# A hybrid encoder step on one core: split weights are kept in DRAM after their first use

## Chip, core and metric

The kernel runs on one core of a Trainium2 chip. Its metric is the device time of one execution in microseconds (us): 2907.6 us before, the median of three runs (2906.4 to 2909.33).

## What is computed

One layer of a streaming encoder is applied to 2048 prompt tokens and 32 sample tokens of width 1024. The parts that matter here, from the reference:

```python
h = _rmsnorm(x, g_mix)
u = h @ w_in                                   # queries, keys, values, pooling input
att = _stick_breaking(q, k_all, v_all, q_pos, k_pos)
x = x + jnp.concatenate([att, pool], axis=-1) @ w_out
h2 = _rmsnorm(x, g_ffn)
x = x + (jax.nn.silu(h2 @ w_ffn_gate) * (h2 @ w_ffn_up)) @ w_ffn_down
gate = jax.nn.sigmoid(_rmsnorm(x, g_ple) @ w_ple_gate)
x = x + (p @ w_ple) * gate
```

w_out and w_ple_gate are 1024 x 1024, w_ffn_gate and w_ffn_up 1024 x 2816, w_ffn_down 2816 x 1024, all float32. A final norm follows.

## The kernel before, in words

**Products in three terms.** Every large product is made from operands split in two float32r parts, hi and lo: `mm3` (lines 204 to 208) issues hi·hi, hi·lo and lo·hi into one PSUM bank. An operand is split by a cast to float32r on ScalarE (ACT), which gives hi, and a subtraction, on VectorE (DVE) with few exceptions on GpSimd (POOL), which gives lo.

**Blocks.** The 2080 tokens are columns. The input projection and pooling branch (`project`) take six blocks of up to 384 columns, the part behind the attention (`rest`) six blocks of 336 or 352, in three pairs each. All blocks of `project` come first. The attention is not a stage of its own: `drive` weaves its steps between the products of the later projections and of the first two pairs of `rest`. In the third pair there is no attention left. One pair of `rest` does, in order: the output projection, one block after the other; the FFN for both blocks together, in groups of up to four chunks of 128 hidden columns; the per-layer embedding with its gate; the final norm, which runs in the background of the next pair. In the last pair the embedding goes one block after the other.

**Weights.** A weight piece is 128 partitions x 1024 elements (0.5 MB). `plan_col` and `plan_down` put pieces into `wplan` in the order of use; `wunit` (lines 183 to 193) hands out one piece and starts the piece after it. A piece is loaded into one of three `wraw` buffers by a DMA from SP's queue (line 95), cast into one of three `whi` (line 190) and subtracted into one of three `wlo` (line 191). A pair of `rest` uses 16 pieces of w_out (eight per block), 22 of w_ffn_gate, 22 of w_ffn_up, 22 of w_ffn_down, and 8 of w_ple_gate (16 in the last pair). So w_out is loaded and split six times and each FFN weight three times. The input projection uses 16 pieces of w_in per pair. A piece of w_out serves 24 matmuls (eight chunks, three terms, one block), a piece of the FFN 48.

**Order of the work.** PE's instructions keep the order in which they are written. The other engines and SP's queue are put in order by the Tile scheduler; each engine then works in order. All DMAs stand in SP's queue: weights, keys and values for the attention (`kt`, `vt`, `q`), the sixteen activation tiles that a pair's output projection starts with (`as<-hx`, line 868), the residual rows (`xs`) and the stores of results. A matmul that needs a PSUM bank waits until its last reader is done; a buffer of a weight is written again when PE has done its last matmul on it.

Of the kernel before, what the change touches and what calls it, by code (L numbers as in the profile page):

```python
# [9 lines left out]
F32 = mybir.dt.float32  # L10
# [7 lines left out]
KC = D // 128  # L18
# [15 lines left out]
# token columns: the 32 sample tokens first, then the prompt.  # L34
# blocks of the input projection (whole tiles of the prompt) and of the rest
# [7 lines left out]
# query groups that a pair of blocks waits for  # L43
# [22 lines left out]
def pieces(c0, n):  # L66
    """Runs of at most 128 tokens in the columns [c0, c0 + n), sample and prompt apart."""
    out, off = [], 0
    if c0 == 0:
        out.append((0, DSEQ))  # L70
        off = DSEQ
    while off < n:
        out.append((off, min(128, n - off)))
        off += 128
    return out
# [3 lines left out]
def stickbreak_step(  # L79
# [35 lines left out]
    # one bank is a third one for transposes while the input projection runs,  # L115
    # and a fourth one for the products after that
# [27 lines left out]
    # gains of the norms, features on partitions  # L144
# [33 lines left out]
    # Weights come in pieces of [128, a, b] with a*b = 1024, in a known order, each  # L178
    # split into two float32r parts; LOOK of them are emitted ahead of their use.
    wplan = collections.deque()  # L180
    wready = collections.deque()

    def wunit():
        while wplan and len(wready) <= LOOK:
            src, a, b, eng = wplan.popleft()
            raw = wpool.tile([128, a, b], F32, tag="wraw", name=nm("wraw"), bufs=RAW_BUFS)
            dma(raw, src)
            hi = wpool.tile([128, a, b], F32R, tag="whi", name=nm("whi"), bufs=W_BUFS)
            lo = wpool.tile([128, a, b], F32R, tag="wlo", name=nm("wlo"), bufs=W_BUFS)
            S.copy(hi, raw)  # L190
            eng.tensor_sub(lo, raw, hi.bitcast(F32))  # L191
            wready.append((hi, lo))
        return wready.popleft()
# [4 lines left out]
    def plan_col(w, c, eng=V):  # L198
        wplan.append((kmaj(w[0, :, c:c + 128]), KC, 128, eng))
# [4 lines left out]
    def mm3(ps, a, b, first=True, last=True):  # L204
        """ps += a.T @ b with a, b = (hi, lo) pairs of APs."""
        T.matmul(ps, a[0], b[0], start=first, stop=False)  # L206
        T.matmul(ps, a[0], b[1], start=False, stop=False)  # L207
        T.matmul(ps, a[1], b[0], start=False, stop=last)  # L208

    # Dense work is a generator that yields PE time; `defer` emits something  # L210
    # after so many further accumulation groups, so that PE does not wait for it.
# [26 lines left out]
    def col_sums(accs, tiles, dim):  # L238
        """accs [128, n]: their sum over partitions, tokens on partitions -> 1/rms [128, nt]."""
        nt = len(tiles)  # L240
        ss = small.tile([128, 4], F32, tag="ss", name=nm("ss"))
        bank = tp_bank()
        if any(wd < 128 for _, wd in tiles):
            GP.memset(ss[:, :nt], 1.0)
        for i, (off, wd) in enumerate(tiles):
            for k, a in enumerate(accs):
                T.matmul(bank[:wd, i:i + 1], a[:, off:off + wd], ones[:, 0:1], start=k == 0, stop=k == len(accs) - 1)
        i = 0
        while i < nt:
            j = i  # L250
            while j < nt and tiles[j][1] == tiles[i][1]:
                j += 1
            wd = tiles[i][1]
            V.tensor_scalar(ss[:wd, i:j], bank[:wd, i:j], 1.0 / dim, EPS, op0=ALU.mult, op1=ALU.add)
            i = j
        return rsqrt_cols(ss, nt)
# [6 lines left out]
    def bcast(r, tiles, n, out):  # L263
        """r [token, tile] -> out [128, n], the same on every partition."""
        bank = tp_bank()
        c0 = tiles[0][0]
        for i, (off, wd) in enumerate(tiles):
            T.matmul(bank[:, off - c0:off - c0 + wd], r[:wd, i:i + 1].broadcast_to([wd, 128]), ident[:wd, :wd],
                     start=True, stop=True)
        S.copy(out, bank[:, :n])  # L270

# [7 lines left out]
    VSC = dram.tile([PAST, NH, 128], F32R, name="vsc")  # L279

# [4 lines left out]
    def rows(c, wd, sample, prompt):  # L285
        """Token rows of a sample / prompt array for the columns from c."""
        if c < DSEQ:
            return sample[c:c + wd, :]
        return prompt[c - DSEQ:c - DSEQ + wd, :]

# [1 line left out]
    halo_prev = [None]  # L292

    def open_block_pair(sup, xpool, pool):
        """The inputs of two blocks: rows on their way, the transposes as a queue to run."""
# [3 lines left out]
        def load_x(b):  # L299
            for i, (off, wd) in enumerate(st["TL"][b]):  # L300
                # the first pair has room where the pooling branch will be
                tag, bufs = ("yt", 2) if b == 1 and i > 0 else ("xn", 4)
                xn = pool.tile([128, D], F32, tag=tag, name=nm("xn"), bufs=bufs)
                dma(xn[:wd, :], rows(st["C0"][b] + off, wd, x_sample[0], x_prompt[0]))
                st["xs"][b].append(xn)
# [34 lines left out]
    def project(sup, pool, st, following):  # L340
        """following() opens the next pair."""
# [33 lines left out]
        for half in range(2):  # L375
            for j in range(2):
                c = 2 * SBW + 256 * half
                wplan.append((kmaj(w_in[0, 512 * j:512 * (j + 1), c:c + 256]), 4, 256, V))
# [6 lines left out]
        # (first column in up, first column of the block, columns)  # L385
# [14 lines left out]
        def pooled(b, g, ps):  # L400
            """The windows of one channel group, from its projection in PSUM; then its map, later."""
# [73 lines left out]
        # the first group goes along with the transposes of x  # L475
# [51 lines left out]
        # values, tokens on partitions  # L527
# [24 lines left out]
        # keys and queries, features on partitions  # L552
# [18 lines left out]
        for c in range(8):  # L571
# [5 lines left out]
            for b in sup:  # L577
# [4 lines left out]
                if last and not isk and c >= HAND_OVER:  # L582
                    # the pools of this phase close as early as possible
                    u = ap.tile([128, WMAX], F32, tag="bot", name=nm("u"), bufs=3)[:, :N[b]]
                    uu = ap.tile([128, 2, WMAX], F32R, tag="aa", name=nm("aa"), bufs=3)[:, :, :N[b]]
                else:
                    u, uu = tmp(b, "u", 3), pair(b)
# [36 lines left out]
    def attn_units(gi, qc, qws, segs):  # L624
        """Per head and key segment of a group of query tiles (columns from qc, widths qws):
        query-tile parts and key-tile parts as closures, in pipeline order."""
# [137 lines left out]
    def attention():  # L764
        """Yields (projections needed, cost) before each slot."""
# [78 lines left out]
    def rest(sup, pool, apool):  # L844
# [7 lines left out]
        def slot(b):  # L852
            """A tile of two float32r parts: [128, 2, N]."""
            return apool.tile([128, 2, OMAX], F32R, tag="as", name=nm("as"), bufs=ACT_SLOTS)[:, :, :N[b]]
# [23 lines left out]
        def ready_h(b, c, key):  # L878
            """X chunk c is final: its squares, and its product with the gain in two parts."""
# [17 lines left out]
        def plan_down(fs):  # L897
            n = 1024 // len(fs)
            for c in range(0, D, n):
                wplan.append((kmaj(w_down[0, fs[0] * 128:(fs[-1] + 1) * 128, c:c + n]), len(fs), n, V))  # L900

        for b in sup:
            for oc in range(KC):
                plan_col(w_out, oc * 128)
        for i, fs in enumerate(groups):
            for f in fs:
                plan_col(w_gate, f * 128)
                plan_col(w_up, f * 128)
# [3 lines left out]
        for i in range(KC if sup != OS[-1] else 2 * KC):  # L912
            plan_col(w_pgate, (i % KC) * 128, V if i else GP)
# [4 lines left out]
        # output projection, one block after the other  # L918
# [18 lines left out]
        # gated FFN  # L937
# [65 lines left out]
        def embed_in(b):  # L1003
            """The embedding's input, transposed."""
# [23 lines left out]
        # per-layer embedding; the last pair goes one block after the other, so that  # L1028
        # the final norm of its first block runs beside the second
# [60 lines left out]
        # the final norm of the last block: the left half of its rows is transposed and  # L1090
        # multiplied by the gain before the sums of squares are known
# [39 lines left out]
        # final norm, back to rows  # L1131
# [89 lines left out]
```

## Time and profile before

| | |
|---|---|
| median of three runs | 2907.6 us (2906.4 to 2909.33) |
| profiled execution, time and span | 2909.9 us, from the first instruction to the last |
| busy: PE, DVE, ACT, POOL | 97%, 70%, 45%, 22% |
| DMA | 366.50 MB in 521919 packets, mean 126 GB/s |
| granted clock of PE | 0.991 of full speed |

Busy time is the time in which at least one instruction of the engine runs. Matmuls overlap, so the mean duration of one (some 320 ns) is longer than the time from one to the next. In the views, L95 is line 95 of the kernel, `whi<-wraw` an instruction that writes a tile whi from a tile wraw, and a wait names the engine that waits, and behind the arrow what ended the wait. PEclk is the share of full clock that TensorE was granted; DMA share is the mean busy share of the core's 16 DMA engines.

### The profile page before, as it was taken

How to read it: one execution, taken by the hardware profiler on the slowest of the kernel's cores; microseconds unless marked ns; L12 is line 12 of the kernel's file. 1: busy time of each engine (PE TensorE's matmuls, PEld its weight loads, DVE VectorE, ACT ScalarE, POOL GpSimd, SP SyncE). 2: the span in 40 equal slices, each digit the busy share in tenths (PEclk: the TensorE clock that was granted, in tenths of full speed). 3: DMA queues.
4: the chain of work that ended last, by engine and by line, in shares of the span. 5: the costliest groups of instructions: out<-in, count | busy, mean ns of one | idle time of the engine just before them, and what ended most of it. 6: DMA issues, size and time to landing. Idle time of an engine off the chain costs nothing.

```text
span 2909.9 us, 50174 instructions
## 1 busy us (share of the span) xinstructions
PE 2829.9 (97%) x18478; PEld 2783.4 (96%) x18478; DVE 2023.3 (70%) x3498; ACT 1302.7 (45%) x2829; POOL 635.8 (22%) x1175
## 2 busy tenths in 40 slices
PE   7989889999999999999999999999999999999998
PEld 6989889989999999998999999999999999999998
DVE  6456689888887787887888777777655644444466
ACT  4454566665444444455554444444343422222243
POOL 2002224223312222232332211212132211111120
PEclk9999999999999999999999999999999999999999
DMA  6775766793333323323563333333225522222223
GB/s 190 207 222 161 188 196 180 219 270 107 98 114 94 104 87 100 109 82 110 185 190 87 90 119 103 105 99 98 82 80 164 172 69 70 67 72 66 73 85 124
DMA packets 521919, 366.50 MB, mean 126 GB/s; under 512 B 62653, under 2 KB 508925, under 8 KB 521674
## 3 DMA queue, kind: packets, MB, share of 16 engines
q1 hardware_dynamic: 521674, 363.30, 42.3%
q8 instruction: 146, 2.39, 0.4%
q14 instruction: 99, 0.81, 0.1%
HBM read 292.89 MB, written 70.32 MB: 125 GB/s over the span
## 4 chain that ended last, share of the span: by engine, by line
PE 81%; DVE 9%; issue 4%; DMA 3%; ACT 2%; POOL 1%; SPq 0%; DVEq 0%; POOLq 0%; ACTq 0%
PE mm L206 23%; PE mm L207 22%; PE mm L208 22%; PE z L694 4%; PE tp L723 4%; PE av L737 2%; PE av L736 2%; DVE keep L712 2%; DVE wlo L191 1%; DVE as L883 1%; DVE win L417 1%; DVE beta L713 1%; ACT whi L190 1%; DVE aa L176 1%; DMA kt<-ks 1%
## 5 line engine op out<-in xcount | busy, mean ns | idle before, releaser
L206 PE MATMUL mm<-as,whi 128*128 128x352 f32 (+1 forms) x3936 | 1299.7, 330 | 2.5 <-DMA as<-hx 2.5
L207 PE MATMUL mm<-as,whi 128*128 128x352 f32 (+1 forms) x3936 | 1264.1, 321 | 0.0
L208 PE MATMUL mm<-as,wlo 128*128 128x352 f32 (+1 forms) x3936 | 1259.3, 320 | 0.0
L206 PEld LDWEIGHTS mm<-as,whi 128*128 128x128 f32 x3936 | 740.9, 188 | 4.9 <-DMA as<-hx 3.8
L207 PEld LDWEIGHTS mm<-as,whi 128*128 128x128 f32 x3936 | 740.9, 188 | 0.3 <-DVE as L883 0.3
L208 PEld LDWEIGHTS mm<-as,wlo 128*128 128x128 f32 x3936 | 740.9, 188 | 0.0
L190 ACT CAST whi<-wraw 128x1024 fp32r<-128x1024 f32 x326 | 342.5, 1051 | 488.7 <-PE mm L207 458.4
L191 DVE TENSOR_TENSOR wlo<-wraw,whi 128x1024 fp32r<-128x1024 f32 x323 | 395.6, 1225 | 79.2 <-ACT whi L190 78.0
L712 DVE TENSOR_TENSOR_SCAN keep<-keep,keep,zeros 128x384 f32<-128x384 f32 (+2 forms) x328 | 315.9, 963 | 115.0 <-ACT keep L697 114.2
L697 ACT ACTIVATE keep<-z 128x384 f32<-128x384 f32 (+3 forms) x464 | 195.8, 422 | 364.7 <-PE z L694 315.0
L967 POOL TENSOR_TENSOR sg<-sg,t 128x352 f32<-128x352 f32 (+1 forms) x132 | 157.9, 1197 | 729.1 <-ACT sg L942 718.2
L713 DVE TENSOR_TENSOR beta<-beta,keep 128x384 f32<-128x384 f32 (+3 forms) x464 | 236.0, 509 | 29.7 <-POOL keep L709 0.5
L709 POOL COPY keep<-keep 128x1 f32<-128x1 f32 (+1 forms) x328 | 149.0, 454 | 437.2 <-DVE keep L712 436.2
L694 PE MATMUL z<-kt,q 128*128 128x384 f32 (+4 forms) x928 | 211.8, 309 | 17.3 <-ACT beta L698 10.7
L176 DVE TENSOR_TENSOR aa<-tp,aa 128x384 fp32r<-128x384 f32 (+4 forms) x472 | 213.0, 451 | 16.5 <-ACT aa L175 15.9
L175 ACT CAST aa<-tp 128x384 fp32r<-128x384 f32 (+4 forms) x472 | 193.1, 409 | 65.6 <-PE tp L723 55.8
L940 DVE TENSOR_TENSOR t<-mm,rbc 128x352 f32<-128x352 f32 (+1 forms) x180 | 92.7, 515 | 162.3 <-PE mm L208 156.8
L206 PE MATMUL mm<-hh,whi 128*128 128x384 f32 (+2 forms) x576 | 202.1, 351 | 3.2 <-ACT acc L447 2.6
L988 DVE TENSOR_TENSOR xs<-xs,mm 128x352 f32<-128x352 f32 (+1 forms) x288 | 144.1, 509 | 85.6 <-PE mm L208 84.9
L723 PE MATMUL tp<-ident,beta 128*128 128x128 f32 (+1 forms) x1112 | 199.0, 273 | 0.6 <-DVE aa L176 0.6
L698 ACT ACTIVATE beta<-z 128x384 f32<-128x384 f32 (+3 forms) x464 | 194.4, 419 | 0.0
L207 PE MATMUL mm<-hl,whi 128*128 128x384 f32 (+2 forms) x576 | 188.9, 328 | 0.6 <-DVE hl L328 0.5
(155 smaller groups left out, 3749.2 us busy)
## 6 DMA issues: line engine op xcount, KB each, us to landing
wraw<-in_w_ffn_gate_dram SPq DMA_DIRECT2D x66, 512.0 KB, 3.9
wraw<-in_w_ffn_up_dram SPq DMA_DIRECT2D x66, 512.0 KB, 3.9
wraw<-in_w_ffn_down_dram SPq DMA_DIRECT2D x66, 512.0 KB, 3.5
wraw<-in_w_in_dram SPq DMA_DIRECT2D x48, 512.0 KB, 4.7
wraw<-in_w_out_dram SPq DMA_DIRECT2D x48, 512.0 KB, 5.3
kt<-ks SPq DMA_DIRECT2D x112, 192.0 KB, 2.4
vt<-vs SPq DMA_DIRECT2D x112, 192.0 KB, 2.8
wraw<-in_w_ple_gate_dram SPq DMA_DIRECT2D x32, 512.0 KB, 3.9
```

Of the source, the lines that this page charges most:

```text
L176: V.tensor_sub(lo, src, hi.bitcast(F32))
L190: S.copy(hi, raw)
L191: eng.tensor_sub(lo, raw, hi.bitcast(F32))
L206: T.matmul(ps, a[0], b[0], start=first, stop=False)
L207: T.matmul(ps, a[0], b[1], start=False, stop=False)
L208: T.matmul(ps, a[1], b[0], start=False, stop=last)
L694: T.matmul(z[:qw, :wi], hd["q"][:, e, qsl], un["k"][:, :wi], start=(e == 0), stop=(e == 1))
L697: S.activation(keep[:qw, :wi], z[:qw, :wi], AF.Sigmoid, scale=-0.125)
L698: S.activation(beta[:qw, :wi], z[:qw, :wi], AF.Sigmoid, scale=0.125)
L712: V.tensor_tensor_scan(rev, rev, zeros[:qw].broadcast_to([qw, wi]), initial=init, op0=ALU.mult, op1=ALU.add)
L713: V.tensor_mul(beta[:qw, :wi], beta[:qw, :wi], keep[:qw, 1:wi + 1])
L723: T.transpose(bank[:kw, qo[i]:qo[i] + qws[i]], un["b"][i][:qws[i], k0:k0 + kw], ident[:qws[i], :qws[i]])
```

## The change

Both parts of a piece now share one tile `w` of 128 x 2 x 1024 elements, again with three buffers. A piece with a key is split at its first use as before, and then stored with both parts (1 MB) in a DRAM tile of its own in `WS2`. When the same key comes again, both parts are loaded straight into `w` (1 MB), with neither a raw load nor a cast nor a subtraction. Keys name the matrix and its first column (for w_ffn_down also its first row chunk), so each of 82 pieces (8 of w_out, 66 of the FFN, 8 of w_ple_gate) is split once; w_in has no keys. The second block of the first pair is the first to load pieces of w_out ready. Comments are removed too.

```diff
     wplan = collections.deque()
     wready = collections.deque()
+    wkept = {}

     def wunit():
         while wplan and len(wready) <= LOOK:
-            src, a, b, eng = wplan.popleft()
-            raw = wpool.tile([128, a, b], F32, tag="wraw", name=nm("wraw"), bufs=RAW_BUFS)
-            dma(raw, src)
-            hi = wpool.tile([128, a, b], F32R, tag="whi", name=nm("whi"), bufs=W_BUFS)
-            lo = wpool.tile([128, a, b], F32R, tag="wlo", name=nm("wlo"), bufs=W_BUFS)
-            S.copy(hi, raw)
-            eng.tensor_sub(lo, raw, hi.bitcast(F32))
-            wready.append((hi, lo))
+            src, a, b, eng, key = wplan.popleft()
+            w = wpool.tile([128, 2, a, b], F32R, tag="w", name=nm("w"), bufs=W_BUFS)
+            if key in wkept:
+                dma(w, wkept[key].rearrange("p c (a b) -> p c a b", a=a))
+            else:
+                raw = wpool.tile([128, a, b], F32, tag="wraw", name=nm("wraw"), bufs=RAW_BUFS)
+                dma(raw, src)
+                S.copy(w[:, 0], raw)
+                eng.tensor_sub(w[:, 1], raw, w[:, 0].bitcast(F32))
+                if key is not None:
+                    wkept[key] = WS2[len(wkept)]
+                    dma(wkept[key].rearrange("p c (a b) -> p c a b", a=a), w)
+            wready.append((w[:, 0], w[:, 1]))
         return wready.popleft()
...
-    def plan_col(w, c, eng=V):
-        wplan.append((kmaj(w[0, :, c:c + 128]), KC, 128, eng))
+    def plan_col(w, c, eng=V, key=None):
+        wplan.append((kmaj(w[0, :, c:c + 128]), KC, 128, eng, key and (key, c)))
...
+    WS2 = [dram.tile([128, 2, 1024], F32R, name=f"ws2_{i}") for i in range(2 * KC + 3 * NF)]
...
-                wplan.append((kmaj(w_in[0, 512 * j:512 * (j + 1), c:c + 256]), 4, 256, V))
+                wplan.append((kmaj(w_in[0, 512 * j:512 * (j + 1), c:c + 256]), 4, 256, V, None))
...
-                wplan.append((kmaj(w_down[0, fs[0] * 128:(fs[-1] + 1) * 128, c:c + n]), len(fs), n, V))
+                wplan.append((kmaj(w_down[0, fs[0] * 128:(fs[-1] + 1) * 128, c:c + n]), len(fs), n, V, ("down", fs[0], c)))
...
-                plan_col(w_out, oc * 128)
+                plan_col(w_out, oc * 128, key="out")
...
-                plan_col(w_gate, f * 128)
-                plan_col(w_up, f * 128)
+                plan_col(w_gate, f * 128, key="gate")
+                plan_col(w_up, f * 128, key="up")
...
-            plan_col(w_pgate, (i % KC) * 128, V if i else GP)
+            plan_col(w_pgate, (i % KC) * 128, V if i else GP, "pgate")
```

## Rows read from the trace of the kernel before

**Rows 1.** The head of the page: span, then busy time and instructions by engine.

```profile
span 2909.9 us, 50174 instructions
...
PE 2829.9 (97%) x18478; PEld 2783.4 (96%) x18478; DVE 2023.3 (70%) x3498; ACT 1302.7 (45%) x2829; POOL 635.8 (22%) x1175
```

**Rows 2.** Busy time by stage; the first line names the columns.

```profile
core 0: us, PE busy (x) PEld busy (x) DVE busy (x) ACT busy (x) POOL busy (x), PEclk, DMA share, GB/s
0.00:535.00 535.00, 484.82 (x3225) 459.90 (x3226) 367.22 (x746) 285.15 (x712) 117.56 (x332) 0.96 0.66 194
535.00:650.00 115.00, 108.45 (x724) 104.00 (x723) 97.73 (x166) 68.49 (x154) 30.44 (x66) 1.00 0.86 253
650.00:1290.00 640.00, 638.49 (x4252) 632.76 (x4251) 510.96 (x853) 307.48 (x681) 162.79 (x312) 1.00 0.35 102
1290.00:1370.00 80.00, 72.59 (x455) 68.65 (x454) 64.84 (x110) 44.74 (x102) 28.91 (x44) 0.96 0.33 97
1370.00:2190.00 820.00, 815.86 (x5343) 809.90 (x5342) 624.45 (x1058) 385.24 (x850) 189.74 (x327) 1.00 0.38 112
2190.00:2775.00 585.00, 585.00 (x3684) 584.73 (x3684) 269.20 (x414) 151.82 (x223) 84.93 (x77) 1.00 0.31 93
2775.00:2910.00 135.00, 124.68 (x808) 123.45 (x806) 88.93 (x156) 59.74 (x109) 21.46 (x20) 0.97 0.36 109
```

**Rows 3.** Groups by line: the split of the weights, on ACT, DVE and POOL.

```profile
L191 DVE TENSOR_TENSOR wlo<-wraw,whi 128x1024 fp32r<-128x1024 f32 x323 | 395.6, 1225 | 79.2 <-ACT whi L190 78.0 <-DMA ks<-uu 0.5 <-issue 0.2
L190 ACT CAST whi<-wraw 128x1024 fp32r<-128x1024 f32 x326 | 342.5, 1051 | 488.7 <-PE mm L207 458.4 <-DMA wraw<-in_w_out_dram 11.7 <-DMA wraw<-in_w_in_dram 11.2
...
L191 POOL TENSOR_TENSOR wlo<-wraw,whi 128x1024 fp32r<-128x1024 f32 x3 | 7.5, 2505 | 0.0
```

**Rows 4.** Waits of PE from 1370 us on: us in total, times, longest.

```profile
PE tp L1009 <- DVE ss L254: 2.4, 2, 1.2
PE tp L268 <- DVE ss L254: 0.8, 1, 0.8
```

**Rows 5.** Busy time in short stretches, columns as in rows 2.

```profile
1311.00:1319.00 8.00, 6.78 (x44) 5.91 (x42) 7.21 (x12) 4.44 (x10) 3.50 (x4) 1.00 0.19 57
1319.00:1327.00 8.00, 4.56 (x18) 3.55 (x17) 5.12 (x11) 2.71 (x8) 2.55 (x5) 0.74 0.50 141
1327.00:1331.00 4.00, 4.00 (x21) 3.90 (x20) 2.05 (x3) 1.35 (x3) 0.00 (x0) 0.67 0.00 0
...
2890.00:2910.00 20.00, 11.12 (x78) 10.45 (x76) 8.87 (x18) 4.44 (x8) 0.85 (x1) 0.83 0.20 72
```

**Rows 6.** Busy time at two output projections, columns as in rows 2.

```profile
585.00:606.00 21.00, 16.99 (x100) 14.38 (x100) 13.86 (x25) 10.32 (x26) 3.94 (x13) 1.00 0.98 329
606.00:632.00 26.00, 25.45 (x170) 25.33 (x171) 24.14 (x37) 17.86 (x38) 9.37 (x16) 1.00 0.99 279
632.00:673.00 41.00, 40.51 (x270) 39.77 (x269) 39.67 (x60) 27.39 (x58) 14.15 (x27) 1.00 0.69 197
2224.00:2301.00 77.00, 77.00 (x502) 76.73 (x501) 52.03 (x73) 33.54 (x52) 21.77 (x21) 1.00 0.77 239
```

**Rows 7.** DMA issues: number, size of each, median us from issue to landing.

```profile
gfin<-in_g_final_dram SPq DMA_DIRECT2D x4, 512.0 KB, 3.7
```

**Rows 8.** Instructions on the tile wraw from 2233 to 2300 us.

```profile
L95 SPq DMA_DIRECT2D wraw<-in_w_out_dram x12: 367/384/1163, 2233.9 to 2280.8; - x12
...
  DMA wraw<-in_w_out_dram: 10.6, 5
...
DMA to landing us min/median/max: 3.8/5.6/8.1
```

**Rows 9.** Waits of SP's DMA queue over the span: us in total, times, longest.

```profile
SPq L95 <- DVE wlo L191: 1058.1, 246, 10.5
```

**Rows 10.** Timeline of PE; in brackets its idle time and who ended it.

```profile
1322.51 2.20 PE L1009 MATMUL tp<-ident,pn 32*128 32x32 f32 x8 [3.44 <-DVE aa L176]
```

## Prediction before the run

> **What bounds the kernel now.** I read the head of the page first. TensorE (PE) is busy for 97% of the span, VectorE (DVE) for 70% [rows 1]. The change takes work from DVE and ScalarE (ACT), so it can pay only where PE waits for those two; the next view must say where PE is idle. Cut by stage, PE is idle for 50 us in the first input projection, 6.6 us at 535 to 650 us, 1.5 us in the FFN of the first pair, 7.4 us at 1290 to 1370 us, 4.1 us in 1370 to 2190 us, nothing from 2190 to 2775 us and 10.3 us at the end [rows 2]. The reader should see that DVE's 624 of 820 us in the second pair cost PE almost nothing: DVE is busy beside PE, not ahead of it. The pure PE rate is in the row of 2190 to 2775 us: 585 us for 3684 matmuls, 159 ns each, without a gap. A weight piece that serves two blocks (48 matmuls) is therefore 7.6 us of PE, one of the output projection (24) 3.8 us.
>
> The span is 2909.9 us [rows 1]; the median of the runs shown is 2907.6 us, 2.3 us less. The sum below is a difference against the profiled span, and I carry it over to the median. About 0.2% (5.8 us) is what a measurement can tell from no change here.
>
> **What the change removes.** 326 pieces are split today [rows 3]; 48 of them belong to w_in and stay. Of the other 278, the first use of each of 82 pieces (8 out, 22 gate, 22 up, 22 down, 8 gate of the embedding) stays split; 196 are loaded ready: 8 in the second block of the first pair, 90 in the second pair, 98 in the third. ACT loses 196 x 1.051 = 206 us, DVE 194 x 1.225 = 238 us, POOL two subtractions of 2.5 us [rows 3]. That is large work with small worth, because PE hides it. The casts run when PE lets go of a slot (458 of their 489 us of idle time ahead of them end on a matmul, [rows 3]), two pieces before the piece is used. What of it lies on the path is bounded by what PE waits for from 1370 us on. The largest entries there are the row sums at the two later embeddings, 2.4 us, and 0.8 us behind them [rows 4]: PE waits for a reduction that stands behind other work on DVE, a subtraction among it. Idle time that is not the final tail is 4.1 + 1.4 us (of the last stage's 10.3 us, 8.9 lie in its last 20 us [rows 2, 5]). So the gain is between 0 and 5.5 us. I take 2.5: the waits for row sums are the only ones where a removed subtraction can be the last thing ahead. Beyond them PE simply stays at its rate.
>
> **What it adds on DMA.** 82 stores of 1 MB and 196 loads of 1 MB instead of 0.5 MB: 86 + 103 = 189 MB more, over 366 MB. The rates that the engines reached while nearly always busy are 329 and 279 GB/s [rows 6], so a 1 MB piece takes 3.2 to 3.8 us of all engines, a 0.5 MB piece now 1.6 to 1.9. Landing: a 0.5 MB load with long rows takes 3.7 us [rows 7]; with another 1.6 us of transfer, 1 MB lands in about 5.3 us when little else moves. The longest landing of a 0.5 MB weight in the crowded stage was 8.1 us [rows 8]; with 1.6 more, 9.7.
>
> **FFN and embedding of the later pairs.** The slot of piece j+3 is freed when PE is done with j, so a load now has two pieces to land: 15.3 us against 5.3 to 9.7. Cost 0. What hides it is the pair of pieces PE still works on. On SP the wait ahead of a load is now for PE's last matmul on a piece instead of a subtraction; behind it stand the kt and vt loads, whose matmuls PE reaches later, and stores. Such waits hold SP for up to 10.5 us already [rows 9], while PE was idle for only 4.1 us in the second pair, so I count nothing for them.
>
> **First pair, FFN and embedding.** Each piece adds a store. On SP the store waits for the subtraction, but the next load of an unsplit piece already waits there for the same kind of subtraction (1058 us in 246 waits, [rows 9]), so kt, vt and q loads queued behind it are held no longer; the extra issue is 0.4 us of SP [rows 8]. The engines are busy for 0.35 there [rows 2]; 66 pieces in 640 us are one in 9.7 us, so the store adds 3.2 to 3.8 in 9.7 and the share becomes about 0.7. I take 0, at most 3 us if a kt load comes late. Slots do not suffer: a store is done long before PE is.
>
> **First pair, output projection.** Here the cover is gone. The engines are busy 0.98 at 585 to 606 us and 0.99 at 606 to 632 [rows 6]: all sixteen activation loads, then the weights that queued behind them. Busy time from 585 to 673 us is 20.6 + 25.7 + 28.3 = 74.6 of 88 us. Added are some six stores of block 0 (6 x 3.2 = 19.2 us) and half a megabyte more for each of the eight loads of block 1 (8 x 1.6 = 12.8). That makes 107, so 19 us too much, if all of it had to be done in there. Some need not be: the last loads may slip into the next stage (share 0.35), and pieces are split some microseconds ahead of use. Bounds 0 and 19 us. I take 4: one store that pushes the first activations (3.2 us), on which PE already waits, and about 1 us for pieces that are split late. It is nearer the low end because the excess is spread over 16 pieces, each with a piece of lead. What is late next is the vt and kt loads of the attention woven in.
>
> **Output projection of pairs two and three.** Pieces are 3.8 us apart in the third pair, so a load has 7.6 us. Landing in 5.3 us would be in time, in 9.7 us it would not. The engines are busy for 0.77 of 2224 to 2301 us, 59 us [rows 6]; 16 x 1.6 = 26 more make 85 of 77 us, but what is over can slip into a stage that is nearly empty, and the longer rows are the cheaper ones. If each load took 9.7 us, three slots would turn over every (9.7 + 3.8) / 3 = 4.5 us: 0.7 us more for each of 16 pieces, 11 us. Bounds 0 and 11; I take 1. In the second pair attention lies between the pieces and spaces them wider; I take 0.
>
> **Sum.** -2.5 + 0 + 0 + 4 + 1 = +2.5 us: 2912.4 as a profiled span, 2910.1, say **2910**, beside the median.
>
> **Rivals.**
> *A, slower: the first output projection starves on the engines.* Mechanism, place and price as above: the stores of block 0 and the doubled loads of block 1 are all needed before 673 us, and PE stands for half to all of the 19 us: 2917 to 2927. It decides as soon as more than some 8 us of the added traffic is ahead of a piece that PE is waiting for. For it: shares of 0.98 and 0.99 with PE at 17 of 21 us. Against: only 0.69 right behind, and PE needs little of what is loaded at once.
>
> *B, slower: ready-split pieces land late in the later output projections.* Price 11 us in the third pair if each lands in 9.7 us: 2907.6 + 11 + 4 - 2.5, about 2920. For it: five casts in that stage already ended a wait for a weight's DMA (10.6 us in all, [rows 8]). Against: cover of one and a half pieces is left unused today, and the median landing is 5.6 us.
> The Trainium skill, "DMA: Bandwidth & Descriptors", section "Bandwidth", speaks for B: its table of measured loads has 1 MB at 6.15 us of busy engines. By that figure the 16 loads would hold the engines for 98 us beside 61 us of PE in the third pair alone, some 37 us lost, as an estimate from that page. The trace disagrees: at the 329 GB/s of its mix loads 1 MB is 3.2 us.
>
> *C, faster by over 0.2%.* At 1319 to 1327 us PE waits 3.4 us for a DVE that is backed up [rows 10], and the granted clock, 1.00 before, is 0.74 in that stretch and 0.67 in the next [rows 5]: some of it is at the lower level of 1.2 GHz. (8 x 0.26 + 4 x 0.33) x 2 = 6.8 us at half rate lose 3.4 us of work. If the new order of DVE's queue ended that stall, 3.4 + 3.4 us and the 5.5 us above come to 12.3: 2895. Against: the subtractions there belong to pieces that the first pair still splits.
>
> That a piece is not found again can't be: keys name matrix and first column, and each repeats unchanged in the later pairs.
>
> **Chances.** Within 0.2% 0.55, A 0.21, B 0.10, C 0.14: faster 0.14, same 0.55, slower 0.31. Range: the forecast's own is 2902 (all 5.5 gained, nothing lost) to 2913 (8 us lost on DMA against 2.5 gained); A and B stretch it to 2924, C to 2900, which leaves most of C and the far end of A outside.
>
> **What would show it.** Right: about 130 casts at L190's place instead of 326, DVE near 1785 us, PE idle unchanged from 1370 us on except for the row sums, and an idle PE or a wait for as<-hx somewhat longer at 585 to 673 us. A shows as PE waits there for a split or for a mix load, with a share of 0.99 up to 673 us. B shows as PE waits for a DMA into w in 2224 to 2301 us. C shows as a gap of under 1 us where 3.4 us stand. I am wrong in kind if PE loses time in the FFN stages, or if the matmul of 159 ns changes.

## The result, and the profile after

The changed kernel takes 2930.5 us (median of 4 runs, 2925.9 to 2934.1) against 2908.5 us of the kernel before in the same session: a ratio of 1.0073 [1.006, 1.0086]. It is slower by 0.7%, past the upper end of the range. The profiled execution is the shortest of the four (2925.9 us, span 2924.2); against the span before [rows 1] it is 14.3 us longer, and against the medians the loss is 22 us. A second profile of the same kernel, further down, shows what the longer ones add.

The head of the page after, and its lines on the new transfers (size of each, median us from issue to landing):

```profile
span 2924.2 us, 49564 instructions
...
PE 2836.0 (97%) x18478; PEld 2788.1 (95%) x18478; DVE 1806.6 (62%) x3304; ACT 1108.3 (38%) x2633; POOL 599.8 (21%) x1173
...
w<-ws SPq DMA_DIRECT2D x196, 1024.0 KB, 5.0
ws<-w SPq DMA_DIRECT2D x82, 1024.0 KB, 5.0
```

The groups of the split by line, after (they answer to [rows 3]):

```profile
L195 DVE TENSOR_TENSOR w<-wraw,w 128x1024 fp32r<-128x1024 f32 x129 | 158.0, 1226 | 39.5 <-ACT w L194 38.2 <-DMA ks<-uu 0.7
L194 ACT CAST w<-wraw 128x1024 fp32r<-128x1024 f32 x130 | 136.5, 1050 | 129.6 <-PE mm L215 113.7 <-DMA wraw<-in_w_in_dram 9.3 <-DMA wraw<-in_w_ffn_gate_dram 2.7
```

The work is gone as planned: 130 casts, DVE at 1806.6 us instead of 2023.3 and ACT at 1108.3 instead of 1302.7. PE does the same 18478 matmuls and ends later. Where it loses is seen by stage and in five short stretches (columns as in [rows 2]):

```profile
535.00:650.00 115.00, 101.29 (x647) 95.61 (x646) 85.07 (x146) 58.27 (x137) 25.61 (x64) 0.96 0.89 286
650.00:1290.00 640.00, 639.53 (x4263) 634.40 (x4262) 507.46 (x851) 304.30 (x679) 162.12 (x308) 1.00 0.70 220
...
1370.00:2190.00 820.00, 813.72 (x5319) 807.57 (x5319) 537.70 (x972) 299.19 (x763) 174.36 (x328) 1.00 0.52 172
2190.00:2775.00 585.00, 581.92 (x3660) 580.63 (x3659) 172.26 (x333) 70.20 (x143) 70.15 (x77) 1.00 0.48 164
...
585.00:606.00 21.00, 17.91 (x108) 15.47 (x108) 14.02 (x27) 9.89 (x25) 4.63 (x13) 1.00 1.02 347
606.00:632.00 26.00, 21.49 (x127) 20.68 (x127) 18.63 (x28) 11.70 (x26) 6.22 (x10) 0.87 0.94 299
632.00:685.00 53.00, 49.87 (x322) 48.78 (x321) 36.07 (x61) 26.44 (x62) 16.46 (x33) 0.97 0.92 304
1716.00:1736.00 20.00, 17.18 (x104) 16.69 (x103) 10.03 (x21) 5.53 (x18) 3.17 (x9) 0.91 0.56 190
2232.00:2320.00 88.00, 84.92 (x546) 83.63 (x545) 32.08 (x59) 19.23 (x39) 19.69 (x22) 1.00 0.90 316
```

In 606 to 632 us PE did 170 matmuls before [rows 6] and does 127 now, at a granted clock of 0.87 where it was 1.00. The share of the engines, which this view can put a little over 1 (1.02 here), is still 0.92 up to 685 us, where it had fallen to 0.69. The FFN of the first pair, with the share up from 0.35 [rows 2] to 0.70, loses nothing. In the second and third pair the two waits of 1.2 us for row sums (tp L1009 <- ss, [rows 4]) are gone, the one of 0.8 us stays, and other waits have come. Waits of PE at 580 to 650 us and from 1370 us on (us in total, times, longest):

```profile
PE mm L213 <- ACT w L194: 5.7, 2, 4.2
PE mm L213 <- DMA as<-hx: 2.3, 5, 1.1
...
PE mm L215 <- DVE w L195: 1.5, 2, 1.2
...
PE mm L213 <- DMA w<-ws: 3.1, 3, 2.5
PE av L744 <- ACT aa L175: 2.7, 1, 2.7
...
PE tp L275 <- DVE ss L261: 0.8, 1, 0.8
```

The timeline shows each at its place (SP's DMA issues and ACT's casts of each place, then PE; in brackets the idle time ahead and who ended it):

```profile
611.52 0.90 SPq L95 DMA_DIRECT2D wraw<-in_w_out_dram  x1
...
614.03 0.49 SPq L95 DMA_DIRECT2D wraw<-in_w_out_dram  x1
...
619.62 1.04 ACT L194 CAST w<-wraw 128x1024 fp32r<-128x1024 f32 x1 [0.15 <-DMA wraw<-in_w_out_dram]
...
633.75 1.07 ACT L194 CAST w<-wraw 128x1024 fp32r<-128x1024 f32 x1
...
1713.02 0.33 SPq L95 DMA_DIRECT2D w<-ws  x1
1714.01 4.06 SPq L95 DMA_DIRECT2D hx<-aa  x3
...
1719.96 0.37 ACT L175 CAST aa<-tp 128x256 fp32r<-128x256 f32 x1 [3.32 <-DMA hx<-aa]
...
620.72 0.65 PE L213 MATMUL mm<-as,w 128*128 128x336 f32 x1 [4.18 <-ACT w L194]
...
634.87 0.42 PE L213 MATMUL mm<-as,w 128*128 128x336 f32 x1 [1.54 <-ACT w L194]
...
636.64 0.65 PE L215 MATMUL mm<-as,w 128*128 128x336 f32 x1 [1.19 <-DVE w L195]
...
1330.72 2.32 PE L1017 MATMUL tp<-ident,pn 32*128 32x32 f32 x8 [3.44 <-DVE aa L176]
...
1720.39 0.38 PE L744 MATMUL av<-aa,vt 128*128 128x256 f32 x1 [2.74 <-ACT aa L175]
...
2289.17 0.43 PE L213 MATMUL mm<-as,w 128*128 128x352 f32 x1 [2.49 <-DMA w<-ws]
```

Before, the casts and the raw load that answer to those of the first place, and the hx stores that answer to the first two of the second place, were:

```profile
606.06 0.43 SPq L95 DMA_DIRECT2D wraw<-in_w_out_dram  x1
...
611.69 1.03 ACT L190 CAST whi<-wraw 128x1024 fp32r<-128x1024 f32 x1
...
619.80 1.05 ACT L190 CAST whi<-wraw 128x1024 fp32r<-128x1024 f32 x1 [1.08 <-DMA wraw<-in_w_out_dram]
...
L95 SPq DMA_DIRECT2D hx<-aa x2: 360/360/360, 1704.1 to 1706.1; - x2
...
DMA to landing us min/median/max: 2.4/2.4/2.4
```

So the loss has three places. **First output projection:** PE waits 5.7 us for casts and 1.5 us for subtractions; the raw pieces behind them were issued and landed late. The piece cast at 611.69 us before is cast at 619.62 now, the one cast at 619.80 at 633.75. The lower clock adds up to 26 x 0.13 + 53 x 0.03 = 5.0 us of lost PE work: 12.2 us at most, since some of the low clock falls into a wait; the table below has 10.7. **1718 us,** in the second pair: PE waits 2.7 us for a split that waits for one of three aa buffers, held by a store of hx; with 20 x 0.09 = 1.8 us for the clock, 4.5. The store that held this buffer before (issued at 1706.1 us) landed in 2.4 us. Now it is issued at 1714.01 us, 1 us behind a ready load of 1 MB, and the split that waits for it starts at 1719.96, 5.9 us later. From 1714 to 1716 us the engines, busy for 0.96, moved none of its rows of 1.5 KB, only packets of 8 KB or more:

```profile
DMA packets 53, 0.43 MB, mean 217 GB/s; under 512 B 0, under 2 KB 0, under 8 KB 0
```

**2289 us,** the third output projection: 3.1 us of waits for ready-split pieces.

The order of the matmuls did not change, so each one's start can be set beside that of the same matmul before. How much the lag grew in each stretch of the time before, in us, for this kernel and for those of the experiments (the one profile of before is the measure, so what shows in nearly all of them alike, as at 670 to 1440 us, isn't read):

```
kernel              0-590 590-670 670-1440 1440-1480 1480-1700 1700-1722 1722-2250 2250-2310 2310-2902
the change           -1.0   10.7    -2.7      1.2      -0.4       4.5      -1.1       4.0      -1.1
change again         -0.3   11.5    -2.0      3.3      -0.4       4.3      -1.1       6.3      -1.1
out split again      -1.0    0.5    -1.3      0.1      -0.4       5.7      -1.2       0.0      -1.1
out kept in block 1  -0.7    1.1    -0.7      1.3      -0.4       4.6      -1.2       2.7      -1.1
stores off SP        -1.4    9.8     4.4      3.5      -0.4       4.7      -1.2       2.6      -1.1
only out kept        -2.9   12.3    -0.5      2.2       0.3       0.0      -0.3       6.0      -0.3
out stored, unread    2.4   12.2    -1.0      0.1      -0.4       4.3      -1.1       0.0      -0.9
small out stores     -5.2    1.4    -1.4      0.1      -0.4       5.6      -1.1       0.0      -1.1
out split, 4 aa      -9.1    0.2    -1.8      3.0      -0.4      -0.4      -1.1       0.3      -1.2
change, 4 aa        -10.5   11.8    -1.5      3.4      -0.4      -0.4      -1.1       7.9      -1.2
before, 4 aa         -8.4   -0.1    -2.0      1.0       0.0      -0.4       0.0       0.2       0.4
change, 4 w           3.3    9.6    -1.7      3.0      -0.4       7.4      -1.1       2.9      -1.1
pgate kept, 4 aa     -9.7    0.3    -2.1      1.4       0.0      -0.4      -1.1       0.0      -0.8
```

### The profile page after: what moved, and what is told of

It reads as the page before. It is cut to its first block, busy times and chain, and to the rows that moved or that the text cites. A ratio compares the mean times of both kernels' runs of the same rounds, so it can differ in the third digit from the quotient of the medians.

```text
span 2924.2 us, 49564 instructions
## 1 busy us (share of the span) xinstructions
PE 2836.0 (97%) x18478; PEld 2788.1 (95%) x18478; DVE 1806.6 (62%) x3304; ACT 1108.3 (38%) x2633; POOL 599.8 (21%) x1173
## 4 chain that ended last, share of the span: by engine, by line
PE 83%; DVE 6%; DMA 4%; issue 3%; ACT 2%; POOL 1%; SPq 1%; DVEq 0%; POOLq 0%; ACTq 0%
PE mm L213 23%; PE mm L214 23%; PE mm L215 23%; PE z L702 4%; PE tp L731 4%; PE av L745 2%; PE av L744 2%; DVE keep L720 1%; DMA w<-ws 1%; DVE win L425 1%; DVE w L195 1%; DVE beta L721 1%; DMA kt<-ks 1%; DVE uu L176 1%; DVE aa L176 1%
## 5 line engine op out<-in xcount | busy, mean ns | idle before, releaser
L213 PE MATMUL mm<-as,w 128*128 128x352 f32 (+1 forms) x3936 | 1301.7, 331 | 11.5 <-ACT w L194 5.7
L214 PE MATMUL mm<-as,w 128*128 128x352 f32 (+1 forms) x3936 | 1265.7, 322 | 0.0
L215 PE MATMUL mm<-as,w 128*128 128x352 f32 (+1 forms) x3936 | 1261.4, 320 | 1.5 <-DVE w L195 1.5
L213 PEld LDWEIGHTS mm<-as,w 128*128 128x128 f32 x3936 | 742.1, 189 | 15.5 <-ACT w L194 6.2
L215 PEld LDWEIGHTS mm<-as,w 128*128 128x128 f32 x3936 | 742.3, 189 | 2.2 <-DVE w L195 2.2
L214 PEld LDWEIGHTS mm<-as,w 128*128 128x128 f32 x3936 | 742.2, 189 | 0.3 <-DVE as L891 0.3
L975 POOL TENSOR_TENSOR sg<-sg,t 128x352 f32<-128x352 f32 (+1 forms) x132 | 135.8, 1028 | 741.4 <-ACT sg L950 727.7
L950 ACT ACTIVATE sg<-t 128x352 f32<-128x352 f32 (+1 forms) x180 | 89.2, 495 | 427.3 <-DVE t L948 427.1
L213 PE MATMUL mm<-hh,w 128*128 128x384 f32 (+2 forms) x576 | 201.9, 351 | 3.6 <-ACT acc L455 3.0
L214 PE MATMUL mm<-hl,w 128*128 128x384 f32 (+2 forms) x576 | 189.1, 328 | 0.6 <-DVE hl L336 0.5
L215 PE MATMUL mm<-hh,w 128*128 128x384 f32 (+2 forms) x576 | 189.1, 328 | 0.4 <-DVE w L195 0.4
```

## The experiments

The theory after the result was rival A with a cause to be found: the bytes of block 0's stores, against the order on SP, the doubled loads of block 1, or the FFN's traffic. Edits are to the changed kernel unless said.

**Out split again.** The output projection is left out of the keeping:

```diff
-                plan_col(w_out, oc * 128, key="out")
+                plan_col(w_out, oc * 128)
```

> w_out has no key: split at each of its six uses, as before; FFN and embedding weights still kept. Theory T1 (the loss sits in the first pair's output projection, 12 us, and in late loads of the third pair's, 3.5 us): both go, 2908 to 2915 us where the change takes 2925 to 2934. Theory T2 (the loss is spread over every stage with 1 MB transfers, such as the 4.5 us behind the store of hx near 1718 us): most of it stays, 2920 us or more.

2911.2 us against 2909.4, ratio 1.0009 [1.0, 1.0018]. By the medians nearly the whole loss goes with 8 of the 82 stores and 40 of the 196 ready loads. In the table 590 to 670 us falls from 10.7 to 0.5 and 2250 to 2310 us from 4.0 to 0; only 1718 us stays.

**Out kept in block 1.** Block 0 splits and stores nothing; block 1 splits and stores:

```diff
+                plan_col(w_out, oc * 128, key=None if b == 0 else "out")
```

> Block 0 of the first pair splits w_out and stores nothing; block 1 splits it once more and stores. T1 by traffic and order in 600 to 640 us: the starved pieces 5 to 7 are in time, 8 or more of the 12 us come back, 2914 to 2921 us. If instead the eight stores and splits only move the stall to block 1 (640 to 680 us): 2922 us or more. T2: no change, 2925 or more.

2922.2 us, 1.0045 [1.0032, 1.0058]. In the profiled execution the same eight stores cost 1.1 us when SP issues them from 625 us on instead of from 568 us on, behind the crowd: there the stage they fall into sets their price. But this execution (span 2915.6 us, 5.7 over) was the fastest of five, and the table shows less than the median's loss. The median lies where the stall was expected to have only moved into block 1; this trace shows no stall there, and where the slower executions lose isn't known.

**Stores off SP.** The stores go to POOL's queue:

```diff
-                    dma(wkept[key].rearrange("p c (a b) -> p c a b", a=a), w)
+                    GP.dma_start(out=wkept[key].rearrange("p c (a b) -> p c a b", a=a).bitcast(F32), in_=w.bitcast(F32))
```

> All 82 stores are issued from GpSimd's queue instead of SP's; the traffic is the same. If the stall in the first output projection is the order on SP (a raw load standing behind a store that waits for a subtraction), raw loads 5 to 7 are issued by 614 us and 6 to 10 us come back: 2917 to 2922 us. If it is the traffic alone: within 3 us of the change, 2925 to 2934.

2937.0 us, 1.0098 [1.0084, 1.0112]: no better than the change, and probably worse (the intervals just touch). SP issues the raw pieces earlier, at 608.06, 611.66 and 616.55 us, and PE still loses 9.8 us; it now waits for activations and a ready piece. Its stretches and its waits of PE at 585 to 690 us:

```profile
585.00:606.00 21.00, 16.68 (x91) 15.21 (x89) 11.00 (x22) 8.21 (x21) 3.55 (x12) 0.84 1.05 370
606.00:632.00 26.00, 24.18 (x157) 22.97 (x156) 20.91 (x33) 14.72 (x33) 10.03 (x17) 1.00 1.07 356
632.00:685.00 53.00, 48.98 (x316) 48.32 (x316) 37.91 (x63) 26.08 (x62) 17.28 (x37) 0.97 0.99 329
...
PE mm L213 <- DMA w<-ws: 4.0, 1, 4.0
PE mm L213 <- DMA as<-hx: 3.7, 2, 3.4
```

The engines run at a share of 1.05, 1.07 and 0.99. So with no store on SP and all the bytes the loss stays; the order on SP chooses which transfer is late. Another 4.4 us go between 670 and 1440 us, most of it in waits of the kind seen at 1718 us: at 830.99 us PE stands 2.66 us for a split of aa that waits for hx stores, and the lag grows by 3.5 us around it.

**Only out kept.** Gate, up, down and the embedding's gate are split each time:

```diff
-                plan_col(w_gate, f * 128, key="gate")
-                plan_col(w_up, f * 128, key="up")
+                plan_col(w_gate, f * 128)
+                plan_col(w_up, f * 128)
...
+            plan_col(w_pgate, (i % KC) * 128, V if i else GP)
```

and so for the pieces of down.

> Only w_out has a key; FFN and embedding weights are loaded and split each time, as before. T1: nearly the whole loss stays, 2920 to 2930 us. T2: most of it goes, 2908 to 2914 us.

2927.8 us, 1.0067 [1.0053, 1.0081]. Out alone does nearly all the harm: 12.3 us in the first output projection and 6.0 in the third. The stall at 1718 us is gone, so that one belongs to the FFN's ready loads; gone too is the gain in the later embeddings (0.3 in place of 1.1, twice).

**Out stored, unread.** Block 0 stores its eight pieces, and every use splits; no load of an out piece is doubled:

```diff
+                plan_col(w_out, oc * 128, key="out" if b == 0 else None)
```

> The kernel of the run with w_out split again (2911 us), but block 0 of the first pair also stores its eight pieces of w_out, 1 MB each, which nothing reads; every use splits. If the stores of block 0 by themselves starve the raw loads of pieces 5 to 7: PE stands 5 to 9 us in 600 to 640 us, 2916 to 2920 us. If it takes the doubled loads of block 1 too: at most 3 us, 2911 to 2914.

2925.1 us, 1.0052 [1.0038, 1.0065], more than expected. The first output projection loses 12.2 us by the stores alone, with the very waits of the change, and the third loses nothing. One stretch and one wait (585 to 690 us):

```profile
606.00:632.00 26.00, 21.29 (x124) 20.45 (x123) 18.78 (x27) 13.03 (x27) 7.04 (x11) 0.87 0.88 301
...
PE mm L213 <- ACT w L194: 5.9, 2, 4.4
```

**Small out stores.** As the last, but each of the eight stores writes 64 KB. It was meant to wait for the same subtraction at the same place on SP, and does neither: `w[:, 0]` is the part that the cast writes, so the store leaves right behind the cast, and SP's order differs too (the first raw load behind the activations is issued at 602.04 us, ahead of the third vt load, where it stood behind it at 615.65 us).

```diff
+                    if key[0] == "out":
+                        dma(wkept[key][:, 0, :128], w[:, 0, 0, :])
+                    else:
+                        dma(wkept[key].rearrange("p c (a b) -> p c a b", a=a), w)
```

> As the run with the unread stores, but each of the eight stores of w_out moves 64 KB instead of 1 MB; it waits for the same subtraction and stands in the same place of SP's queue. If the bytes are the cause: no stall, 2910 to 2913 us. If the wait on SP is the cause: as with full stores, 2916 to 2920.

2913.4 us, 1.0012 [1.0003, 1.0021]. The stretch that the last run lost is whole again; below it, one piece's cast, store and subtraction:

```profile
606.00:632.00 26.00, 25.27 (x170) 24.59 (x169) 24.01 (x36) 17.60 (x39) 9.87 (x16) 1.00 0.93 260
...
618.23 1.07 ACT L194 CAST w<-wraw 128x1024 fp32r<-128x1024 f32 x1
...
619.32 0.32 SPq L95 DMA_DIRECT2D ws<-w  x1
...
619.64 1.22 DVE L195 TENSOR_TENSOR w<-wraw,w 128x1024 fp32r<-128x1024 f32 x1
```

170 matmuls at full clock, as before [rows 6]: 1.4 us lost in place of 12.2. So eight more issues on SP don't make the loss. This run alone can't part the stores' bytes from their wait for a subtraction and their place on SP, as all three changed; the run with the stores off SP, which kept the bytes and took wait and place off SP, lost 9.8 us. Together they point to the bytes. No run changed the bytes alone.

**Out split, four aa.** The first experiment, with a fourth aa buffer; a slot of X makes room:

```diff
-ACT_SLOTS, X_SLOTS = 26, 20
+ACT_SLOTS, X_SLOTS = 26, 19
...
-            aa = ap.tile([128, 2, w], F32R, tag="aa", name=nm("aa"), bufs=3)
+            aa = ap.tile([128, 2, w], F32R, tag="aa", name=nm("aa"), bufs=4)
```

(and so at the two other places of aa).

> The kernel with w_out split again, with four buffers for the tile aa instead of three (room for it: 19 instead of 20 buffers of residual rows). If the wait at 1718 us comes from a buffer of aa that a store of hx holds while a 1 MB weight load is ahead of it, the 4.6 to 5.6 us go: 2904 to 2907 us, 2 to 5 us under the kernel before. If the stall has another cause: 2910 to 2913.

2900.5 us, 0.9967 [0.9956, 0.9979]. At 1718 us 5.7 becomes -0.4: the buffer was what PE lacked. Unexpected are 9 us gained before 590 us (in the runs with three aa this column goes from -5.2 to 3.3).

**Change, four aa.** The same edit on the full change.

> The full change with four buffers of aa and 19 of residual rows. Same theory: 4 to 6 us less than the change's 2926 to 2934, with the stalls in the first and third output projection as they were (some 12 and 3 us): 2921 to 2929 us. If the stall at 1718 us has another cause: 2926 to 2934.

2920.9 us, 1.0039 [1.0027, 1.0051]. Again the stall at 1718 us is gone and some 10 us are gained before 590 us, and the first (11.8) and third (7.9) output projections stay.

**Before, four aa.** The same edit on the kernel before, to price the buffer by itself.

> The kernel before, every weight split at each use, with four buffers of aa and 19 of residual rows. If the 9 us that the run with w_out split again and four aa gained on the kernel before come from the buffers alone: 2899 to 2903 us, and keeping the FFN weights is worth less than 2 us either way. If they come from the kept weights together with the buffers: 2906 us or more.

2903.8 us, 0.9978 [0.9969, 0.9987]. The gain ahead of 590 us (8.4) comes with this edit (one buffer of aa more, one of X less) and owes nothing to the change.

**Change, four w.** A fourth slot gives a ready piece 3.8 us more lead in the third pair:

```diff
-RAW_BUFS, W_BUFS, LOOK = 3, 3, 1
+RAW_BUFS, W_BUFS, LOOK = 2, 4, 1
...
-BETA_BUFS = 7
+BETA_BUFS = 6
...
+ACT_SLOTS, X_SLOTS = 26, 19
```

> The full change with four buffers of w instead of three (room for them: two raw buffers instead of three, six of beta instead of seven, 19 of residual rows). If the waits for ready-split pieces in the third output projection (3.1 us) come from a lead of only two pieces, they fall under 0.5 us there; with the stores of the first pair unchanged the stall at 600 to 640 us stays at 8 us or more. In sum 2920 to 2930 us, the smaller beta uncertain. If the engines' bytes alone set these waits: 3 us or more remain in the third pair.

2933.5 us, 1.008 [1.0067, 1.0094]. A miss: the wait in the third pair did not go below 0.5 us. Waits of PE at 2232 to 2330 us, and the stretch:

```profile
PE mm L213 <- DMA w<-ws: 2.3, 2, 2.0
...
2232.00:2320.00 88.00, 85.73 (x552) 84.69 (x551) 32.74 (x61) 19.26 (x39) 19.89 (x22) 1.00 0.86 309
```

2.3 us in place of 3.1. One more piece of lead does little, which makes the engines' time (0.86 to 0.90 over 88 us) the likelier cause; no run took bytes out of that stage alone, so it isn't shown. As the other buffers shrank too, the rest of this run can't be read.

**Only the embedding's gate kept, four aa.** The part that can pay without harm: w_ple_gate keeps its key, out and FFN lose theirs, aa has four buffers.

> Four buffers of aa, 19 of residual rows, and only the eight pieces of w_ple_gate kept; out and FFN weights are split at each use. If the gain of kept weights is the two waits for row sums at the later embeddings (1.15 us each), this has all of it without the stores of the FFN: 1 to 3 us under the kernel before with four aa, 2897 to 2901 us. If the gain needs the FFN's splits gone too: the same as that kernel.

2900.0 us, 0.9971 [0.9958, 0.9983]. It has the gain of the later embeddings (1.1 and 0.8 us) without the FFN's 66 stores. Its interval overlaps those of the two other kernels with four aa that split out each time; all three beat both the kernel before and the change, and which is best isn't settled.

**Change again.** No edit; a second profile, as the first was of the shortest run.

> The change itself, once more, beside the kernel before on one chip, because its four runs lie in two pairs, 2926 and 2934 us, and only one at 2926 left a trace. If the three stalls of that trace (some 12, 4.5 and 3.4 us, less 2.3 of gain) are the whole effect: a median 15 to 20 us over the kernel before, 2923 to 2930 us, and the same three places in the trace. If there is another cost that its trace happened to miss: 2931 us or more, and a fourth place in this trace.

2931.2 us, 1.0076 [1.0062, 1.009]; the profiled execution has a span of 2930.6 us, 20.6 over. The three places are back (11.5, 4.3, 6.3), and one that was small in the first profile has grown to 3.3 us, at 1440 to 1480 us. DVE, then PE, in its timeline:

```profile
1468.54 0.99 DVE L942 TENSOR_TENSOR xs<-xs,mm 128x352 f32<-128x352 f32 x2 [2.21 <-DMA xs<-xt]
...
1475.06 0.84 PE L1104 MATMUL tp<-ident,xs 128*128 128x128 f32 x4 [2.22 <-DVE aa L176]
```

A load of 176 KB is issued at 1461.66 us right behind a ready piece of 1 MB and lands 6.9 us later. DVE stands at it in order, and the splits behind it, which PE wants, come late. Here the granted clock also falls at this place (0.83 in 1475 to 1485 us) and in the third pair (0.98 in 2232 to 2320 us), which it did not in the first profile. DVE waits for xs at this place in the first profile too (1.1 us), with the stores off SP (2.4) and with four w (2.0), and neither in the kernel before nor with out split again. But out split with four aa loses 3.0 us there through another wait, so the place isn't the change's alone. The longer executions, then, mostly pay the same waits, a little longer and more often with a lower clock behind them.

## Why the prediction was wrong

- **First pair, output projection: the step that failed.** "Bounds 0 and 19 us. I take 4": it measured 10.7 and 11.5 in the two profiles of the change. Rival A had mechanism, place and price right (half to all of 19 us). Two errors. The argument for the low end, that the excess "is spread over 16 pieces, each with a piece of lead", fails: five of block 0's stores are issued in the stretch whose share was already 0.98 and 0.99 [rows 6], and the delay falls on a few pieces (7.9 and 14.0 us for the two above), each with a lead of 3.8 us. By themselves the stores cost 12.2 us. The doubled loads of block 1, 12.8 of the 32 us in the sum, were not needed for it. And the sum had no term for the clock behind a wait, which made up to 5.0 us of the loss, though [rows 5] show that very loss at 1319 us and the prediction priced it, for rival C alone.
- **"FFN and embedding of the later pairs ... Cost 0": failed.** The ready pieces do land in time there, but other transfers wait behind them. An hx store of 384 KB that landed in 2.4 us before holds its aa buffer for 5.9 us behind a 1 MB load and costs 4.5 us at 1718 us. Before, a raw load of 0.5 MB stood behind the first two hx stores; one store behind it took 5.2 us, and PE waited for none. The prediction asked how long SP is held and counted "nothing for them"; it did not ask which buffers a transfer holds while it stands behind a big one.
- **Output projections of pairs two and three.** For the third, 1 us was taken and 4.0 to 6.3 measured, within the bounds of 0 and 11. For the second 0 was taken and 1.2 to 3.3 measured, at 1440 to 1480 us: not the pieces but xs behind them, as far as that place is the change's. Rival B's reason, too little lead, isn't borne out (a fourth slot took 0.8 us off the wait), though that run shrank other buffers too.
- **FFN of the first pair: right.** A share near 0.7 was forecast and is 0.70; PE is idle for 0.5 us where it was 1.5.
- **The gain: right.** 2.5 us taken, 1.1 + 1.1 measured, at the later embeddings; of the waits for row sums [rows 4] those of 2.4 us are gone. "Large work with small worth": 194 us less of ACT and 217 less of DVE bought 2.2 us. Casts (130) came as forecast, and DVE (1806.6, forecast 1785) nearly.
- **Rival C did not happen.** The stall is still 3.44 us [rows 10].
- **The price of 1 MB.** Estimated at 3.2 to 3.8 us of all engines and a landing of 5.3; the median landing is 5.0, and the stretch of 585 to 606 us moves 347 GB/s, 3.0 us for each MB. The Trainium skill's "DMA: Bandwidth & Descriptors", section "Bandwidth", lists 6.15 us for 1 MB loads issued from GpSimd; by it the third pair would lose some 37 us, as an estimate from that page. The runs disagree: the change loses 4.0 to 6.3 us there.

The chances put 0.55 on no change. A alone (10.7 less 2.2 for the gain, on 2907.6: some 2916) would have been inside the range; with 4.5 us at 1718 us, 4.0 in the third pair and what the longer executions add it is not. Cases that I had set side by side, A and late pieces, came together.

## What to carry to other kernels

Work that the bound engine hides pays only what that engine now waits for, here 2 us out of 400 removed; read that from its waits before anything else. Price added DMA bytes in the stage they fall into: the same eight stores cost 12 us where the engines' share was near 1, and 1 us behind that stretch, in the one profile of it. Ask too what small transfers now land behind the big ones and which buffers those hold, and add to each new wait of PE the lower clock that can follow it.

## What was not expected of the hardware

- A short wait of PE can be followed by a lower granted clock, and need not be. After 4.18 us it was 0.87 over 26 us, after 2.74 us 0.91 over 20 us; after 2.49 us in the third pair it stayed 1.00, and after 2.76 us at the same place in the second profile it was 0.98 over 88 us (1.8 us of work lost, as in the 20 us at 0.91).
- Stores on POOL's queue raised the rate: 370 GB/s over 21 us and 356 over the next 26, against 347 and 299 with the same stores on SP's queue. PE gained nothing by it.
- A fourth aa buffer, with one X buffer less, is worth 5.3 us to the kernel before by the medians (2903.8 against 2909.1); in the table it gains 8.4 us ahead of 590 us, where attention runs beside the input projection. Which wait it takes away there wasn't tried.
